# Fewer gather steps among the gate groups and eight modulation rows moved, in the second expert layer of a decoder trunk

## The chip, the cores and the metric

The kernel runs on one core of a Trainium2 chip. The metric is device time in microseconds, the median of several runs. The engines of the core are named as in the profile: PE is the matrix engine (PEld its weight load), DVE the vector engine, ACT the scalar engine, POOL the general-purpose engine, and SP issues transfers. Transfers are also issued from ACT and POOL; all run on the same 16 transfer engines.

## The reference

A small decoder trunk with 512 tokens of width 1024 and two layers. The first layer mixes tokens with a gated linear recurrence, the second with latent attention; each is followed by an expert layer ("peer"), which is what this case is about. Every sub-layer is normalised and modulated by shift, scale and gate vectors computed from a conditioning vector c.

```python
mod = (jax.nn.silu(c) @ ada_w[l] + ada_b[l])[:, None, :]
sh1, sc1, g1, sh2, sc2, g2 = jnp.split(mod, 6, axis=-1)
...
h = rmsnorm(x, norm_ffn_g[l]) * (1.0 + sc2) + sh2
x = x + g2 * peer(h, ...)

def peer(h, w_q, sub_keys, u_tab, v_tab):
    q = (h @ w_q).reshape(B, S, PEER_HEADS, 2, PEER_HALF)
    s = jnp.einsum('bshpd,hpnd->bshpn', q, sub_keys)
    v1, i1 = lax.top_k(s[..., 0, :], PEER_TOPK)
    v2, i2 = lax.top_k(s[..., 1, :], PEER_TOPK)
    ...
    idx = e1 * N_KEYS + e2
    g = jax.nn.softmax(cv, axis=-1)
    act = gelu(einsum('bcd,bchkd->bchk', hc, u_tab[ic]))
    out = einsum('bchk,bchkd->bcd', gc * act, v_tab[ic])
```

Each token picks 16 of 16384 experts in each of 8 heads, 128 experts in all. An expert is one row of u (a dot product with the token) and one row of v (added with the gated activation as its factor).

## The kernel before

Tokens are handled in four blocks of 128. For three of them (384 tokens) the expert layer is computed densely: the tables u and v are streamed in 128 tiles of 128 experts, PE multiplies every token with every expert, and a matrix of gates, zero where a token did not pick an expert, selects. The fourth block is computed by gathering: for each of its 128 picks a row of u and a row of v is fetched per token, and DVE does the arithmetic.

The function `peer(l)` runs for l = 0 and l = 1, in these stages:

- **Scoring.** Four rounds of query products (pq), key products (sc) and top-k searches on DVE. After each round some modulation rows are computed (`adas`, line 1181: six in the first layer, two in the second) and some u parts run on PE. In the last round the fourth block is decoded at once, so that gathering can begin.
- **u parts** (`u_part`). One streams a tile of u, splits it into a high part (whi, on ACT) and a low part (wlo, on DVE, line 165), runs 24 products of 384 columns on PE (lines 201 to 203) and keeps the activations (gact). They fill every stage until all 128 are done; 66 of them are parked in memory (gscr). Each of the 8 blocks of the width takes three products (high and low parts), for precision.
- **Gate groups** (`gate_group`, line 1009 on). 24 groups of 16 tokens. For each half group DVE builds two one-hot tiles (oo, line 1022) and their product with the gates (pr, line 1024); PE multiplies them (wps, 8 pairs per half group) into gate matrices; ACT evicts those and they are written to memory (wscr). u parts stand between the groups. Two more blocks are decoded on DVE during this stage.
- **Value tiles.** For each of 128 tiles t: the gates are read back (wt), the activations weighted (line 1239) and split (ah on ACT, al on DVE), the tile of v loaded and split (vh on ACT, vl on DVE), and 18 products of 512 columns accumulate on PE (acc). From tile 76 to tile 110 each tile also carries one u part.
- **Close.** The second layer's output is turned to token order, normalised and stored.

**Gather steps** (`gather_steps`, line 1441 on) are a generator of 256 steps for the fourth block. Each step fetches one row per token into a slot named grow (four slots) with an indirect transfer on POOL's queue (line 1451). The steps come in rounds of 32: sixteen with rows of u, each a dot product on DVE (line 1455), then sixteen with rows of v, each a scaled sum into gacc on DVE (line 1460, the very first one line 1458). `EARLY` of the 256 are taken among the gate groups: after group i the count is brought up to `EARLY * (i + 1) // 20`, so that it is complete after the twentieth of 24 groups. The rest is spread over the value tiles by weights (`plan`): in the second layer 0.2 for tiles 0 to 7, 0.6 for 8 to 75, 2.6 for 76 to 110, 1.0 for 111 to 125.

**Modulation rows** (`ada`, line 145 on). There are 112 rows of 128 outputs. For each one its weights are loaded (ada_raw, 512 KB) and DVE multiplies them with the conditioning vector and sums (ada_junk, line 153), into one column of mod. `self.todo` lists the rows that are left and `adas` takes the next ones. The last eight, 88 to 95, are the gate g2 of the second expert layer; their first reader is `token_major` at value tile 90. In the first layer the value tiles take a row at every third tile from 38 on, with its load on POOL's queue and into a grow slot.

What sets the order: each engine works through its own queue in order, and waits there on semaphores. The order in a queue is made when the program is built, by a scheduler that simulates a timeline and keeps to the data dependences and to the `issue_after` hints, which place an instruction behind a given one. So an edit at one place can shift the order of its neighbours.

Of the kernel before, what the change touches and what calls it, by code (L numbers as in the profile page):

```python
# [46 lines left out]
UDEC = 13  # L47
UEND = 7
QUIET = 4
EARLY = 74  # L50
HT = 8
RAWS = 4
GROWS = 4
# [30 lines left out]
class Trunk:  # L84
# [953 lines left out]
    def peer(self, l):  # L1038
        nc, io, tc = self.nc, self.io, self.tc
        nd = NB - 1  # L1040
        with ExitStack() as st:
# [67 lines left out]
            def u_part(after=None):  # L1109
                t = state["u"]  # L1110
                state["u"] = t + 1
                out = self.bank("u", True)
                hi, lo = self.wtile(io["uT"][l][t], KC, eng=nc.vector)
                with tc.issue_after(after) if after is not None else ExitStack():
                    for k, (bh, bl) in enumerate(h):
                        self.mm3(out[:, :ND], (hi[:, k, :], lo[:, k, :]), (bh[:, :ND], bl[:, :ND]), k == 0, k == KC - 1)
                if t < OWN:
                    gact[t] = self.x.rearrange("p k t -> p (k t)")[:, t * ND:t * ND + ND]
                elif LEAD - SPILL <= t < LEAD:
                    g = acts.tile([P, ND], F32, name="gsp", bufs=3)  # L1120
                    nc.scalar.activation(g, out[:, :ND], AF.Gelu)
                    nc.scalar.dma_start(self.gscr[l, t - (LEAD - SPILL)], g)
                    return
                else:
                    gact[t] = ring(t)
                nc.scalar.activation(gact[t], out[:, :ND], AF.Gelu)  # L1126

            gpool = st.enter_context(tc.tile_pool(name=f"gath{l}", bufs=1))
# [6 lines left out]
            done = 0  # L1135
# [4 lines left out]
            def decodes(bs):  # L1140
                for b in bs:
                    res = []
                    for _ in self.decode(dpool, cvs[b], cis[b], iu[b], res):
                        yield
                    if b == nd:
                        gsel.append(self.gather_index(gpool, l, *res))
                    else:
                        prep[b] = self.gate_prep(pool, *res)

            with tc.tile_pool(name=f"pq{l}", bufs=1) as pool:  # L1150
                for grp in range(4):
                    keys = pool.tile([P, 4, P], F32, name="keys", bufs=2)
                    nc.scalar.dma_start(keys, io["keysT"][l][:, 4 * grp:4 * grp + 4, :])
                    outs = []
                    wq = l * 16 + 4 * grp
                    if grp == 0:
                        outs = pq0
                    qs = []
                    for m in range(4):
                        if m >= len(outs):  # L1160
                            outs.append(self.bank("pq"))
                            self.lin(outs[m], self.wtile(io["w_pq"][wq + m], KC, eng=nc.vector), h)
                        q = pool.tile([P, T], F32, name="pq_s", bufs=5)
                        nc.scalar.activation(q, outs[m], AF.Copy)
                        qs.append(q)
                    for b in (nd, *range(nd)):
                        sc = self.bank("sc")
                        for m in range(4):
                            nc.tensor.matmul(sc[:, m * P:m * P + P], qs[m][:, b * P:b * P + P], keys[:, m, :],
                                             start=True, stop=True)  # L1170
                        for m in range(4):
                            last = self.topk_half(pool, sc[:, m * P:m * P + P], vs[b][:, 4 * grp + m, :],
                                                  iu[b][:, 4 * grp + m, :])
                        self.candidates(pool, vs[b], cvs[b], cis[b], 2 * grp, 2)
                        if grp == 3 and b == nd:
                            for _ in decodes((nd,)):
                                pass
                            gsteps = self.gather_steps(gpool, l, *gsel[0], hn)
                    self.hold = ()
                    with tc.issue_after(last):  # L1180
                        self.adas(6 if l == 0 else 2, pool)
                    for _ in range(UPQ[grp]):
                        u_part()
            with tc.tile_pool(name=f"gate{l}", bufs=1) as pool:
                nsg = P // TG
                steps = decodes(range(nd))
                for i in range(UDEC):
                    u_part()
                while 0 not in prep:
                    next(steps)  # L1190
                n0, nt = state["u"], nd * nsg
                ds = 0
                wlast, plast = [None, None], []
                for i in range(nt):
                    more = 1 if i >= nsg and i % nsg < nsg // 2 else 0
                    while state["u"] < n0 + (LEAD - UEND - n0) * (i + 1) // nt + more:
                        u_part(after=wlast[-2])
                    w, p = self.gate_group(pool, l, i // nsg, i % nsg, *prep[i // nsg])
                    wlast.append(w)
                    plast.append(p)  # L1200
                    while ds < 7 * (i + 2) // nsg:
                        next(steps, None)
                        ds += 1
                    with tc.issue_after(plast[max(0, i - 1)]):
                        while done < min(EARLY, EARLY * (i + 1) // (nt - QUIET)):
                            next(gsteps)
                            done += 1
                while state["u"] < LEAD:
                    u_part(after=wlast[-1])
# [71 lines left out]
            for t in range(P):  # L1281
                j = t + RING - 3
                if t >= OWN and j < P:
                    if j < LEAD:
                        gact[j] = ring(j)
                        nc.sync.dma_start(gact[j], self.gscr[l, j - (LEAD - SPILL)])
                    else:
                        u_part()
                if t == P - 2:
                    late = vp.tile([P, NSG, WG * TG], F32R, name="late", tag="wt").rearrange("p a b -> p (a b)")  # L1290
                pair = weigh(t), v_load(t)
                if acc is None:
                    acc = [[self.bank(f"acc{b}{f}") for f in range(2)] for b in range(nd)]
                if t < P - LAST:
                    for f in range(2):
                        grp["v"] = v_part(t, f, *pair)
                else:
                    held.append((t, pair))
                if l == 0 and t == 2:
                    self.positions(gpool)  # L1300
                if l == 0 and 36 <= t < 84 and t % 3 == 2:
                    with tc.issue_after(grp["i"].ins):
                        self.adas(1, gpool, 64, GROWS, nc.gpsimd, "grow")
                if t >= 20 and (t - 20) % 8 == 0 and (t - 20) // 8 < KC:
                    k = (t - 20) // 8
                    with tc.issue_after(vdma[t]):
                        nc.sync.dma_start(self.x[:, k, :], self.xscr[:, k, :])
                if l == DEPTH - 1 and t >= 26 and (t - 26) % 8 == 0 and (t - 26) // 8 <= KC:
                    with tc.issue_after(grp["v"]):
                        self.token_major((t - 26) // 8, g2)  # L1310
                if l == DEPTH - 1 and t == P - 12:
                    fg = hpool.tile([P, D], F32, name="fgrow", tag="h4")
                    with tc.issue_after(vdma[t]):
                        nc.sync.dma_start(fg, bass.AP(tensor=io["final_g"].tensor, offset=io["final_g"].offset,
                                                      ap=[[0, P], [1, D]]))
                with tc.issue_after(grp["i"].ins):
                    while done < min(total, int(goal[t] + 0.01)):
                        next(gsteps)
                        done += 1
# [26 lines left out]
            for t, pair in held:  # L1346
                last = v_part(t, 0, *pair)
            self.preload(AF.Sqrt, emit(0))
            rest, c = None, 0
            for q in range(2):  # L1350
                for i, (t, pair) in enumerate(held):
                    with tc.issue_after(last):
                        last = v_part(t, 1, *pair, 2 * q * P, 2 * P, rest)
# [3 lines left out]
                    for _ in range((0, 2, 1, 1, 1, 0)[LAST * q + i]):  # L1357
                        with tc.issue_after(last):
                            last = finish(c)
# [196 lines left out]
```

## Time and profile before

| | us |
|---|---|
| median of 3 runs | 2970.81 |
| the runs | 2964.76, 2970.81, 2972.43 |
| the profiled execution | 2963.21 |
| its span, first to last instruction | 2961.4 |

| stage of the second expert layer, in the profiled execution | us from the span's start |
|---|---|
| scoring | from about 1715 |
| first gather step's transfer | 1952 |
| gate groups | 1975 to 2247 |
| remaining u parts | to 2278 |
| value tiles, first to last product | 2278 to 2952 |

A profile is one execution. Its page gives the busy time of each engine and the chain of work that ended last. The table of windows gives busy time per stage. Views of groups, waits and the timeline show single instructions: their start, their duration, and what ended the idle time before them. Durations of instructions that follow each other overlap a little, so the distance between starts is the better measure of what an instruction costs its engine.

### The profile page before, as it was taken

The numbers are of one execution on the slowest core, as the hardware profiler recorded it, in microseconds if no ns is written. First come the engines' busy times: TensorE is split into PE (matmuls) and PEld (weight loads), VectorE is DVE, ScalarE is ACT, GpSimd is POOL, SyncE is SP. The second block draws the span as 40 slices with busy tenths as digits, with TensorE's granted clock in tenths as the row PEclk, the third lists the DMA queues.
The fourth block names the chain that finished last, engine by engine and source line by source line (L and its number), as shares of the span: only waits on it lengthen the run. The fifth ranks groups of instructions, "written<-read, shape, count | busy, mean of one in ns | idle before, by whom it ended". The sixth has DMA issues, their size and how long they took to land.

```text
span 2961.4 us, 43899 instructions
## 1 busy us (share of the span) xinstructions
PE 2874.9 (97%) x15680; PEld 2566.0 (87%) x15680; DVE 2559.4 (86%) x4887; ACT 1387.6 (47%) x2039; POOL 960.9 (32%) x718
## 2 busy tenths in 40 slices
PE   7999999989999999999999999999999999999998
PEld 5689898989888889998778799999989888899997
DVE  8989999999888878889878888999997777888888
ACT  4753245656343333333576742456655333333333
POOL 4000003645142234535434400015643111244542
PEclk9999999999999999999999999999999999999999
DMA  8544558999999999999323334369999999999996
GB/s 317 188 139 147 173 178 305 357 371 367 307 393 359 365 321 354 319 350 324 121 83 114 120 132 136 125 216 353 362 355 370 319 335 322 310 328 354 345 333 224
DMA packets 296219, 813.71 MB, mean 275 GB/s; under 512 B 33152, under 2 KB 130560, under 8 KB 289600
## 3 DMA queue, kind: packets, MB, share of 16 engines
q1 hardware_dynamic: 188928, 439.41, 43.4%
q0 software_dynamic: 78912, 287.34, 26.9%
q10 hardware_dynamic: 28160, 84.14, 7.3%
q8 instruction: 124, 2.03, 0.3%
q14 instruction: 95, 0.78, 0.1%
HBM read 727.44 MB, written 83.36 MB: 274 GB/s over the span
## 4 chain that ended last, share of the span: by engine, by line
PE 72%; DVE 15%; issue 5%; DMA 4%; POOL 2%; ACT 2%; ACTq 0%; DVEq 0%; SPq 0%; POOLq 0%
PE acc L202 11%; PE acc L203 11%; PE acc L201 11%; PE u L201 8%; PE u L202 8%; PE u L203 8%; DVE wlo L165 3%; POOL grow L1451 2%; DVE oo L1022 1%; DMA grow<-in_u_dram,idx 1%; DVE pr L1024 1%; PE pq L202 1%; PE pq L203 1%; DMA ada_raw<-in_adaw_dram 1%; PE pq L201 1%
## 5 line engine op out<-in xcount | busy, mean ns | idle before, releaser
L1451 POOL DMA_INDIRECT grow<-in_u_dram,idx x256 | 374.8, 1464 | 1099.2 <-DVE gdot L1455 404.4
L201 PE MATMUL u<-h,wlo 128*128 128x384 f32 x2048 | 692.8, 338 | 2.0 <-DVE wlo L165 1.0
L203 PE MATMUL u<-h,whi 128*128 128x384 f32 x2048 | 688.5, 336 | 0.0
L202 PE MATMUL u<-h,whi 128*128 128x384 f32 x2048 | 687.6, 336 | 0.0
L203 PE MATMUL acc<-vh,ah 128*128 128x512 f32 x1512 | 589.4, 390 | 0.0
L202 PE MATMUL acc<-vl,ah 128*128 128x512 f32 x1512 | 589.1, 390 | 0.0
L1451 POOL DMA_INDIRECT grow<-in_v_dram,idx x256 | 411.6, 1608 | 514.5 <-DVE gacc L1460 336.5
L201 PE MATMUL acc<-vh,al 128*128 128x512 f32 x1512 | 555.8, 389 | 0.0
L165 DVE TENSOR_TENSOR wlo<-raw,whi 128x1024 fp32r<-128x1024 f32 (+1 forms) x313 | 383.3, 1226 | 85.0 <-ACT whi L164 84.9
L165 DVE TENSOR_TENSOR vl<-vraw,vh 128x1024 fp32r<-128x1024 f32 x252 | 308.4, 1224 | 125.8 <-ACT vh L164 120.5
L164 ACT ACTIVATE whi<-raw 128x1024 fp32r<-128x1024 f32 (+2 forms) x362 | 352.4, 975 | 114.9 <-issue 33.2
L201 PEld LDWEIGHTS u<-h,wlo 128*128 128x128 f32 x2048 | 386.6, 189 | 6.1 <-ACT gact L1126 1.7
L202 PEld LDWEIGHTS u<-h,whi 128*128 128x128 f32 x2048 | 386.3, 189 | 2.7
L203 PEld LDWEIGHTS u<-h,whi 128*128 128x128 f32 x2048 | 385.8, 188 | 0.1
L203 PEld LDWEIGHTS acc<-vh,ah 128*128 128x128 f32 x1512 | 283.8, 188 | 59.2
L202 PEld LDWEIGHTS acc<-vl,ah 128*128 128x128 f32 x1512 | 283.8, 188 | 57.4
L201 PEld LDWEIGHTS acc<-vh,al 128*128 128x128 f32 x1512 | 283.8, 188 | 57.0
L1460 DVE SCALAR_TENSOR_TENSOR gacc<-grow,gdot,gacc 128x1024 f32<-128x1024 f32 x254 | 325.2, 1280 | 8.9 <-DMA grow<-in_v_dram,idx 7.8
L1455 DVE CUSTOM_DVE_ANT_0 grow<-grow,hn 128x1024 f32<-128x1024 f32 x256 | 309.7, 1220 | 20.9 <-DMA grow<-in_u_dram,idx 20.6
L164 ACT ACTIVATE vh<-vraw 128x1024 fp32r<-128x1024 f32 x252 | 264.6, 1050 | 97.0 <-issue 73.5
L164 ACT ACTIVATE ah<-gact 128x384 fp32r<-128x384 f32 x204 | 106.6, 523 | 390.0 <-PE acc L203 248.5
L1033 ACT ACTIVATE stg<-wps 128x512 f32<-128x512 f32 x192 | 185.0, 1120 | 40.4 <-PE wps L193 40.4
(417 smaller groups left out, 4342.9 us busy)
## 6 DMA issues: line engine op xcount, KB each, us to landing
raw<-in_uT_dram SPq DMA_DIRECT2D x256, 512.0 KB
vraw<-in_v_dram SPq DMA_DIRECT2D x256, 512.0 KB
wscr<-stg ACTq DMA_DIRECT2D x48, 1024.0 KB
wt<-wscr SPq DMA_DIRECT2D x42, 1024.0 KB
ada_raw<-in_adaw_dram SPq DMA_DIRECT2D x76, 512.0 KB
gscr<-gsp ACTq DMA_DIRECT2D x132, 192.0 KB
gact<-gscr SPq DMA_DIRECT2D x108, 192.0 KB
ada_raw<-in_adaw_dram POOLq DMA_DIRECT2D x36, 512.0 KB
```

What stands on the lines that cost most here:

```text
L164: last = nc.scalar.activation(hi, src, AF.Copy)
L165: lo = (eng or nc.vector).tensor_tensor(lo, src, hi.bitcast(F32), op=OP.subtract)
L201: nc.tensor.matmul(out, al, bh, start=first, stop=False, **kw)
L202: nc.tensor.matmul(out, ah, bl, start=False, stop=False, **kw)
L203: last = nc.tensor.matmul(out, ah, bh, start=False, stop=last, **kw)
L1022: nc.vector.tensor_tensor(oo.rearrange(by_pair, d=2), io, toks(et), op=OP.is_equal)
L1024: prod = nc.vector.tensor_tensor(pr.rearrange(by_pair, d=2), hot, toks(gp), op=OP.mult)
L1033: nc.scalar.activation(stg[:, :, c:c + 4].rearrange("p e t -> p t e"), wps.rearrange("p (t e) -> p t e", t=4), AF.Copy, scale=1.0 / GSCALE)
L1451: nc.gpsimd.indirect_dma_start(out=row, out_offset=None, in_=tabs[s], in_offset=bass.IndirectOffsetOnAxis(ap=idx[:, k:k + 1], axis=0))
L1455: nc.vector.tensor_tensor_reduce(row, row, hn, op0=OP.mult, op1=OP.add, scale=1.0, scalar=0.0, accum_out=col)
L1460: nc.vector.scalar_tensor_tensor(acc, row, col, acc, op0=OP.mult, op1=OP.add)
```

## The change

Three edits, all for the second layer (l = 1):

- `EARLY` becomes a pair: 74 for the first layer as before, 56 for the second. Eighteen gather steps are therefore taken in the value tiles instead of among the gate groups.
- The two modulation rows after each scoring round are dropped for l = 1.
- The value tiles of the second layer also take a modulation row at every third tile from 38 on, while there are any left (eight: tiles 38 to 59), with its load on POOL's queue and into a grow slot.

```diff
-EARLY = 74
+EARLY = (74, 56)
...
                     self.hold = ()
-                    with tc.issue_after(last):
-                        self.adas(6 if l == 0 else 2, pool)
+                    if l == 0:
+                        with tc.issue_after(last):
+                            self.adas(6, pool)
                     for _ in range(UPQ[grp]):
                         u_part()
...
                     with tc.issue_after(plast[max(0, i - 1)]):
-                        while done < min(EARLY, EARLY * (i + 1) // (nt - QUIET)):
+                        while done < min(EARLY[l], EARLY[l] * (i + 1) // (nt - QUIET)):
                             next(gsteps)
                             done += 1
...
                 if l == 0 and t == 2:
                     self.positions(gpool)
-                if l == 0 and 36 <= t < 84 and t % 3 == 2:
+                if 36 <= t < 84 and t % 3 == 2:
                     with tc.issue_after(grp["i"].ins):
-                        self.adas(1, gpool, 64, GROWS, nc.gpsimd, "grow")
+                        self.adas(1, gpool, (64, 112)[l], GROWS, nc.gpsimd, "grow")
```

## The prediction

> **What bounds the kernel now.** I read four views: the page for the whole, a table of windows cut at the stages of the second expert layer, the groups and waits of its gate stretch, and the timeline. The page first:
>
> ```profile
> PE 2874.9 (97%) x15680; PEld 2566.0 (87%) x15680; DVE 2559.4 (86%) x4887; ACT 1387.6 (47%) x2039; POOL 960.9 (32%) x718
> PE   7999999989999999999999999999999999999998
> GB/s 317 188 139 147 173 178 305 357 371 367 307 393 359 365 321 354 319 350 324 121 83 114 120 132 136 125 216 353 362 355 370 319 335 322 310 328 354 345 333 224
> PE 72%; DVE 15%; issue 5%; DMA 4%; POOL 2%; ACT 2%; ACTq 0%; DVEq 0%; SPq 0%; POOLq 0%
> ```
>
> PE carries the chain, with DVE close behind. But a share of the span does not say where an edit pays; the stages do. The table of windows of the second expert layer (columns: window, length, then busy time of each engine with its instructions in brackets, granted clock, share of the transfer engines, GB/s):
>
> ```profile
> core 0: us, PE busy (x) PEld busy (x) DVE busy (x) ACT busy (x) POOL busy (x), PEclk, DMA share, GB/s
> 1740.00:1890.00 150.00, 150.00 (x819) 138.56 (x818) 129.67 (x643) 46.12 (x62) 0.00 (x0) 1.00 0.41 130
> 1890.00:1920.00 30.00, 30.00 (x178) 30.00 (x177) 29.55 (x158) 14.81 (x19) 0.00 (x0) 1.00 0.33 106
> 1920.00:1950.00 30.00, 30.00 (x175) 30.00 (x174) 29.86 (x113) 15.66 (x21) 0.00 (x0) 1.00 0.46 144
> 1950.00:1975.00 25.00, 25.00 (x147) 24.93 (x146) 23.18 (x54) 14.67 (x21) 5.29 (x4) 1.00 0.80 270
> 1975.00:2247.00 272.00, 256.46 (x1932) 250.32 (x1930) 261.11 (x310) 169.53 (x211) 147.75 (x69) 0.97 0.95 348
> 2247.00:2278.00 31.00, 30.49 (x186) 30.45 (x187) 16.64 (x22) 13.78 (x20) 7.94 (x5) 1.00 1.05 365
> 2278.00:2574.00 296.00, 296.00 (x1319) 245.10 (x1318) 223.38 (x292) 109.73 (x153) 47.23 (x50) 1.00 0.94 326
> 2574.00:2887.00 313.00, 313.00 (x1579) 283.25 (x1578) 261.88 (x334) 115.49 (x157) 149.75 (x114) 1.00 0.94 337
> 2887.00:2961.00 74.00, 65.86 (x290) 53.94 (x288) 66.48 (x92) 28.99 (x51) 21.50 (x14) 0.96 0.61 226
> ```
>
> 1740 to 1890 is scoring: PE full, DVE with 20 us to spare. 1975 to 2247 holds the gate groups: the only long stage where PE is not full and DVE nearly is (261.1 of 272). From 2278 the value tiles run, cut here at tiles 72 and 112: PE full in both rows, DVE free for 73 and 51 us.
>
> How much does PE really lose in the gate stretch? A busy PE need not run at its pace, so I take the pace from starts. Timeline, one undisturbed piece, first and last of 32 gate products and of 45 u products:
>
> ```profile
> 2046.96 0.23 PE L1030 MATMUL wps<-pr,oo 128*128 128x128 f16 x1
> 2048.70 0.22 PE L193 MATMUL wps<-pr,oo 128*128 128x128 f16 x1
> 2049.41 0.33 PE L201 MATMUL u<-h,wlo 128*128 128x384 f32 x1
> 2057.04 0.34 PE L203 MATMUL u<-h,whi 128*128 128x384 f32 x1
> ```
>
> 31 steps in 1.74 us are 0.056 us each; 44 in 7.63 us are 0.1734. The tables of windows for tile u and for tile wps give the counts of the gate stretch:
>
> ```profile
> 1975.00:2247.00 272.00, 213.81 (x1174) 204.93 (x1172) 24.23 (x49) 0.97 0.95 348
> 1975.00:2247.00 272.00, 52.13 (x752) 88.68 (x93) 0.97 0.95 348
> ```
>
> 1174 x 0.1734 + 752 x 0.056 = 245.7 us. So PE loses 272 - 245.7 = **26.3 us**, 15.5 of it plainly idle, the rest below pace (the granted clock is 0.97 there). The stretch's waits of PE and of DVE name the cause:
>
> ```profile
> PE wps L1030 <- DVE pr L1024: 15.1, 7, 5.1
> DVE grow L1455 <- DMA grow<-in_u_dram,idx: 5.0, 3, 4.4
> DVE wlo L165 <- ACT whi L164: 3.8, 3, 2.7
> DVE oo L1022 <- PE wps L193: 2.1, 2, 1.2
> ```
>
> PE waits for pr, the gate product's operand that DVE makes; DVE itself waits 10.9 us in all. The stretch is bound by DVE.
>
> **The change part by part.** *Eighteen gather steps leave the gate groups.* The groups of grow in that stretch:
>
> ```profile
> L1455 DVE CUSTOM_DVE_ANT_0 grow<-grow,hn x37: 1212/1222/1227, 1982.4 to 2241.7; 128x1024 f32<-128x1024 f32 x37
> L1460 DVE SCALAR_TENSOR_TENSOR gacc<-grow,gdot,gacc x31: 1240/1281/1289, 2043.5 to 2222.3; 128x1024 f32<-128x1024 f32 x31
> ```
>
> Steps alternate 16 dots (L1455) and 16 sums (L1460). 74 steps end 10 dots into the third round, 56 end 8 sums into the second round: 8 sums and 10 dots leave. What a step holds DVE is its distance to the next start:
>
> ```profile
> 1983.58 1.22 DVE L1455 CUSTOM_DVE_ANT_0 grow<-grow,hn 128x1024 f32<-128x1024 f32 x1
> 1984.73 1.22 DVE L1455 CUSTOM_DVE_ANT_0 grow<-grow,hn 128x1024 f32<-128x1024 f32 x1
> 2910.54 1.28 DVE L1460 SCALAR_TENSOR_TENSOR gacc<-grow,gdot,gacc 128x1024 f32<-128x1024 f32 x1
> 2911.74 0.55 DVE L165 TENSOR_TENSOR al<-gact,ah 128x384 fp32r<-128x384 f32 x1
> ```
>
> 1.15 and 1.20 us, so 10 x 1.15 + 8 x 1.20 = 21.1 us, about one step per group, since the quota is spread over twenty groups. DVE's work falls to 261.1 - 21.1 = 240.0 us; with its 10.9 us of waits kept, 250.9. PE needs 245.7. The two bounds now lie 5 us apart, and work cut so finely does not interleave perfectly, so I take 254: **18 us gained**. The ends: 26.3 us (no PE loss left) and 6.4 (the loss falls only as the steps do, 26.3 x 18/74). The longest single wait should shrink too; DVE's timeline there:
>
> ```profile
> 1998.70 1.23 DVE L1455 CUSTOM_DVE_ANT_0 grow<-grow,hn 128x1024 f32<-128x1024 f32 x1 [4.43 <-DMA grow<-in_u_dram,idx]
> 2000.99 2.35 DVE L1024 TENSOR_TENSOR pr<-oo,gp 128x2048 f16<-128x2048 f16 x2
> ```
>
> A dot stood before pr and waited for a row, as the first two groups ask for seven rows of four slots. They will ask for five. What is late next is PE itself, or a remaining decode before pr.
>
> *Eight modulation rows leave scoring.* Each takes 1.28 us of DVE:
>
> ```profile
> L153 DVE CUSTOM_DVE_ANT_0 ada_junk<-ada_raw,csil,vecs x8: 1277/1280/1295, 1778.1 to 1938.3; 128x1024 bf16<-128x1024 f32 x8
> ```
>
> 10.2 us go from a stage where PE is full at 1.00 clock, so the cover is PE and I count nothing. The last two stand at 1935 and 1938, where DVE has no pause; decoding may end 2.5 us earlier. That can only shorten the first gate wait, within the 26.3. SP loses eight loads of 512 KB at a transfer share of 0.41: nothing.
>
> *Both arrive at the value tiles.* There 200 steps instead of 182 are spread by the weights, whose sum over the tiles is 148.4 (8 x 0.2 + 68 x 0.6 + 35 x 2.6 + 15 x 1.0): 0.81 a tile instead of 0.74 up to tile 75, 3.50 instead of 3.19 in tiles 76 to 110 (where u parts run too), 1.35 instead of 1.23 in 111 to 125. The rows take every third tile from 38 to 59. DVE gets 4.9 steps and eight rows by tile 72, 16 us into 73 free; 11.3 steps by tile 112, 13 us into 51 free, and is then busy 275 of 313, 88%. Each brings a transfer of 128 x 1024 x 4 bytes, 0.524 MB, on POOL's queue, busy 47 and 150 us of 296 and 313. A row's load takes a grow slot, so the next gather queues behind it on POOL, and vl and al behind it on DVE. Can PE keep its pace under that? The first layer already does this with 182 steps and 16 rows (here 200 and 8); its value tiles, up to tile 31, 71 and 111:
>
> ```profile
> 760.00:890.00 130.00, 130.00 (x575) 107.63 (x574) 113.45 (x164) 51.94 (x70) 44.44 (x30) 1.00 1.00 363
> 890.00:1054.00 164.00, 164.00 (x725) 135.84 (x724) 134.44 (x185) 59.42 (x82) 43.37 (x40) 1.00 1.00 364
> 1054.00:1365.00 311.00, 311.00 (x1561) 281.51 (x1560) 255.52 (x327) 112.39 (x154) 139.11 (x108) 1.00 0.93 332
> ```
>
> DVE at 87% in the first row, and PE full in all; its weights give up to 3.26 steps a tile, so 3.50 lies somewhat beyond. Second-layer traffic would be 326 + 12.9 x 0.524 MB / 296 us = 349 GB/s, then 337 + 11.3 x 0.524 / 313 us = 356. Only the 90 us of tiles 38 to 59 go higher: 9.6 transfers more, 326 + 56 = 382. The first layer's slice from 814 to 888 us moved 393 with PE at nine tenths or more. So I count **nothing**; the ends are nothing (PE is already full, no gain possible) and 41 us, the whole 26 transfers at 332 GB/s.
>
> *The end.* 1.8 more steps in tiles 111 to 125, 2.1 us of DVE, into a stretch where it works 66.5 of 74 us; the last sum must precede the last token block. I take 0.5 us, ends 0 and 2.1.
>
> Sum: -18 + 0 + 0 + 0.5 = -17.5 us. The profiled execution took 2963.2 us (span 2961.4), so 2945.7 on its scale; it lies 7.6 us under the median of three, 2970.8, the scale of the forecast: **2953.3 us**.
>
> **The rivals.**
>
> *Order, not load.* PE's waits come from single orders in DVE's queue (a dot whose row has not landed, a burst of decode) and survive. For it: the 4.43 us above. Against it: DVE waits 10.9 us in 272, while 21 us of work go. Gain 6.4 - 0.5: 2964.9 us.
>
> *Transfers bound the value tiles.* If they already run at what the queues deliver, each added transfer delays the value loads: 26 x 0.524 MB = 13.6 MB at 332 GB/s cost 41 us, against 18 gained: 2970.8 + 23 = 2993.8 us. It decides once the deliverable rate lies below 349 to 356; the gain is used up at about 344. For it: the share of 0.94. Against it: 363 and 364 in the first layer, and the value tiles' own waits of DVE on rows:
>
> ```profile
> DVE grow L1455 <- DMA grow<-in_u_dram,idx: 7.2, 8, 2.5
> ```
>
> *A cap in tiles 38 to 59 alone.* If nothing above the 364 GB/s of the first layer can be held for long, 382 is 18 too much for 90 us: 18 x 90 / 364 = 4.5 us, 2957.8 us. For it: both first-layer stages stop at the same figure. Against it: the slice of 393. The Trainium skill, "DMA: Bandwidth & Descriptors", section "Bandwidth", gives such a cap, a memory limit of about 358 GB/s for one core; by it the estimate is 24 x 90 / 358 = 6 us, 2959.3 us. The trace disagrees with that figure: two stages ran at 363 and 364 for 294 us with PE full.
>
> *The change does less than it says.* Were fewer than eight rows left, the value tiles would carry fewer; the eight L153 rows exclude it, and the first use of them is at tile 90, after 59.
>
> **How the numbers follow.** Forecast 0.60, the cap 0.06, order 0.20, transfers 0.10 (with half their price, no change, 0.04 more). The low end is the full 26.3 us below the lowest run shown, 2964.8: 2938.5. The high end takes in the order rival and a value stretch that gives some back: 2970. About 0.3%, 9 us, is what a measurement of this kernel can tell from no change. Faster 0.60 + 0.06 = 0.66, same 0.20 + 0.04 = 0.24, slower 0.10.
>
> **What would show it.** Right: the gate stretch near 254 us, its PE loss under 10 us, pr waits of PE near a third of 15.1; the value tiles from first to last product still 675 us with PE full; DVE near 88% in tiles 76 to 110. Wrong: pr waits that stay with DVE idle (order), or value tiles where PE waits for vl or al behind a grow or ada_junk that waits for DMA (transfers). A reordered DVE queue elsewhere in the layer would also break it.

## The result and the profile after

The changed kernel takes 2986.12 us (median of 5 runs, 2984.34 to 2993.76) against 2970.55 us before in the same comparison: a ratio of 1.0065, 95% interval 1.005 to 1.0081. It is slower. The forecast was 2953.3 us, the range 2938.5 to 2970, and 0.10 stood on slower.

The profiled execution of the changed kernel took 2993.76 us (span 2992.0), the slowest of its five. Of the 30.6 us between its span and that of before, 10.4 lie ahead of the second layer's first query product (1714.1 us before, 1724.5 after), where PE, DVE and POOL work in the same order in both traces: that is how executions differ, not the change. So I compare lengths of stages, cut at the first and last product of each kind:

| us | scoring (first pq to first wps) | gates and rest of u (to first acc) | value tiles (to last acc) | after the last product |
|---|---|---|---|---|
| before | 270.1 | 293.4 | 674.8 | 9.0 |
| after | 271.5 | 285.7 | 677.6 | 32.6 |
| difference | +1.4 | -7.7 | +2.8 | **+23.6** |

The gate stretch gained 7.7 us, the value tiles lost 2.8, and 23.6 appeared where nothing was before: behind the last product. The page of the changed kernel, engines and chain:

```profile
PE 2881.8 (96%) x15680; PEld 2571.9 (86%) x15680; DVE 2560.7 (86%) x4887; ACT 1389.3 (46%) x2041; POOL 949.8 (32%) x726
PE 73%; DVE 14%; issue 5%; DMA 4%; ACT 2%; POOL 2%; ACTq 0%; DVEq 0%; SPq 0%; POOLq 0%
```

On the page the two kernels cannot be told apart; the chain by engine moves by one per cent. The table of windows by stage can (columns as in the prediction):

```profile
1755.00:1900.00 145.00, 145.00 (x784) 133.68 (x783) 121.90 (x629) 43.00 (x58) 0.00 (x0) 1.00 0.34 110
1990.00:2252.00 262.00, 251.09 (x1926) 244.15 (x1925) 244.50 (x286) 166.36 (x207) 115.95 (x56) 0.99 0.93 340
2282.00:2578.00 296.00, 296.00 (x1318) 245.10 (x1317) 235.12 (x320) 109.18 (x151) 62.28 (x63) 1.00 0.96 343
2578.00:2891.00 313.00, 313.00 (x1578) 283.28 (x1577) 258.67 (x319) 114.72 (x158) 143.21 (x110) 1.00 0.93 331
2960.00:2992.00 32.00, 0.00 (x0) 0.00 (x0) 21.67 (x30) 7.25 (x21) 5.48 (x6) 0.57 0.52 185
```

The fourth row is the one to look at. Tiles 72 to 112 were to get 11.3 gather steps more; DVE does 319 instructions there against 334 before, and the transfers move 331 GB/s against 337. More was asked and **less** was done, with PE full all the time. The last row is where the missing steps are: 32 us without a product, DVE at work in 21.7 of them. DVE's timeline there, lines left out between:

```profile
2945.47 2.60 DVE L1461 SCALAR_TENSOR_TENSOR gacc<-grow,gdot,gacc 128x1024 f32<-128x1024 f32 x2
...
2964.11 3.98 DVE L1461 SCALAR_TENSOR_TENSOR gacc<-grow,gdot,gacc 128x1024 f32<-128x1024 f32 x3
2969.24 1.28 DVE L1461 SCALAR_TENSOR_TENSOR gacc<-grow,gdot,gacc 128x1024 f32<-128x1024 f32 x1 [1.16 <-DMA grow<-in_v_dram,idx]
2971.98 1.28 DVE L1461 SCALAR_TENSOR_TENSOR gacc<-grow,gdot,gacc 128x1024 f32<-128x1024 f32 x1 [1.45 <-DMA grow<-in_v_dram,idx]
2973.58 2.60 DVE L1461 SCALAR_TENSOR_TENSOR gacc<-grow,gdot,gacc 128x1024 f32<-128x1024 f32 x2 [0.32 <-DMA grow<-in_v_dram,idx]
2976.22 1.29 DVE L1392 TENSOR_TENSOR y<-gacc,csil 128x512 f32<-128x512 f32 x2
```

The last product starts at 2959.4; sums (L1461, L1460 before) run on to 2976.2, some of them waiting for their rows, and then the fourth block is still to be normalised and stored, 15.8 us with nothing beside it. Before the change the last sum started at 2934.2, so all of this lay beside PE. The chain of the last stretch agrees; it goes from a slot to a transfer to a slot (start, length, what):

```profile
2953.24 1.82 POOL grow L1452
...
2955.64 5.79 DMA grow<-in_v_dram,idx
...
2967.83 5.66 DMA grow<-in_v_dram,idx
...
2973.58 1.29 DVE gacc L1461
```

That the steps are late is not an accident of the last tiles. DVE works its queue in order, so counting the steps ahead of each tile's weighting (L1240) in the trace gives the order of that queue:

| steps ahead of the weighting of tile | 72 | 80 | 88 | 96 | 104 | 112 | 120 | 127 |
|---|---|---|---|---|---|---|---|---|
| before | 123 | 138 | 164 | 189 | 214 | 235 | 247 | 256 |
| after | 109 | 124 | 149 | 172 | 197 | 218 | 230 | 240 |

From tile 80 to 104 the weights ask for 24 x 3.5 = 84 steps; 73 stand there, fewer than the 76 of before. Sixteen are left behind the last weighting. That is the order as built, and the chip keeps up with it. In tiles 72 to 112 PE waits for nothing, and DVE waits for rows no longer than this (us in total, times, longest):

```profile
DVE grow L1456 <- DMA grow<-in_u_dram,idx: 2.3, 1, 2.3
DVE gacc L1461 <- DMA grow<-in_v_dram,idx: 2.2, 2, 1.5
```

The 2.8 us of the value tiles are the first of the late steps: PE stops twice after 2945, 2.4 us in all, for an `al` that stands behind sums in DVE's queue. Last, the waits of PE and DVE in the gate stretch:

```profile
DVE wlo L165 <- ACT whi L164: 10.9, 10, 3.1
PE wps L1030 <- DVE pr L1024: 8.0, 8, 3.9
DVE oo L1022 <- PE wps L193: 3.0, 2, 2.0
DVE grow L1456 <- DMA grow<-in_u_dram,idx: 1.7, 2, 1.0
```

PE's waits for pr fell from 15.1 to 8.0 us, but not to a third; DVE idles 17.5 of 262 us now.

### The profile page after: what moved, and what is told of

It is laid out like the page before. It is cut to its first block, busy times and chain, and to the rows that moved or that the text cites. A ratio compares the mean times of both kernels' runs of the same rounds, so it can differ in the third digit from the quotient of the medians.

```text
span 2992.0 us, 43923 instructions
## 1 busy us (share of the span) xinstructions
PE 2881.8 (96%) x15680; PEld 2571.9 (86%) x15680; DVE 2560.7 (86%) x4887; ACT 1389.3 (46%) x2041; POOL 949.8 (32%) x726
## 4 chain that ended last, share of the span: by engine, by line
PE 73%; DVE 14%; issue 5%; DMA 4%; ACT 2%; POOL 2%; ACTq 0%; DVEq 0%; SPq 0%; POOLq 0%
PE acc L203 11%; PE acc L202 11%; PE acc L201 11%; PE u L201 9%; PE u L203 9%; PE u L202 9%; DVE wlo L165 2%; POOL grow L1452 2%; DMA ada_raw<-in_adaw_dram 1%; PE pq L202 1%; PE pq L201 1%; PE pq L203 1%; PE wps L1030 1%; DVE ada_junk L153 1%; PE wps L193 1%
## 5 line engine op out<-in xcount | busy, mean ns | idle before, releaser
L1452 POOL DMA_INDIRECT grow<-in_u_dram,idx x256 | 357.0, 1394 | 1082.4 <-DVE gdot L1456 383.0
L1461 DVE SCALAR_TENSOR_TENSOR gacc<-grow,gdot,gacc 128x1024 f32<-128x1024 f32 x254 | 325.1, 1280 | 12.7 <-DMA grow<-in_v_dram,idx 11.6
```

What stands on the lines that cost most here:

```text
L1452: nc.gpsimd.indirect_dma_start(out=row, out_offset=None, in_=tabs[s], in_offset=bass.IndirectOffsetOnAxis(ap=idx[:, k:k + 1], axis=0))
L1461: nc.vector.scalar_tensor_tensor(acc, row, col, acc, op0=OP.mult, op1=OP.add)
```

## The experiments

All diffs are against the changed kernel; each ratio is to the kernel before, in the same comparison.

**The two halves apart.** `only_gather` moves the steps and leaves the rows in scoring; `only_rows` does the reverse.

```diff
 # only_gather
-                    if l == 0:
-                        with tc.issue_after(last):
-                            self.adas(6, pool)
+                    with tc.issue_after(last):
+                        self.adas(6 if l == 0 else 2, pool)
...
-                if 36 <= t < 84 and t % 3 == 2:
+                if l == 0 and 36 <= t < 84 and t % 3 == 2:
 # only_rows
-EARLY = (74, 56)
+EARLY = (74, 74)
```

> Theories for the 16 to 22 gather steps that the changed kernel still has to do when PE's last product ends. Order: DVE's queue was built with only about 3.1 steps a tile in tiles 76 to 110 although the quota is 3.5, so the steps stand behind the last tile's work before the chip starts. Ring: on the chip four slots with a round trip of 11.0 us allow only 0.36 steps per us. Transfers: the value tiles run at what the transfer engines deliver. Here the eight modulation rows are back in scoring and the 18 steps stay in the value tiles. Order: the queue as built has 11 steps behind the last weighting instead of 16, so about 5 x 1.5 us less at the end, 2978 us. Ring: the rows are far from the tiles that are short of slots, so nothing changes, 2986. Transfers: 8 of 26 transfers less, 13 us, 2973.

> The eight rows in the value tiles, but 74 steps among the gate groups as before. Order: one step behind the last weighting, so the end is as before, 2970 us within 5, if the rows cost nothing by themselves. Ring: the same. Transfers: 8 x 0.524 MB at 332 GB/s, 13 us, 2983.

`only_gather`: 2978.00 us, ratio 1.002 (1.0009 to 1.003); 11 steps behind the last weighting, 21.0 us after the last product. `only_rows`: **2962.72 us, ratio 0.9967 (0.9954 to 0.9979)**, 9.0 us after the last product, value tiles 674.8. So the moved steps make the tail; the rows alone make the kernel faster. What the halves gain in front, over scoring and gates together: 3.1 us the steps alone (563.5 to 560.4), 6.9 the rows alone (556.6), 6.3 both (557.2). Each value is from one execution, and kernels with the same queues differ by up to 3.6 us in this part (below), so whether the gains add cannot be told. The gate stretch of `only_rows`, then of `only_gather`, in the table of windows:

```profile
1986.00:2248.00 262.00, 251.00 (x1937) 244.20 (x1936) 257.93 (x303) 167.60 (x209) 154.29 (x67) 0.99 0.98 359
```

```profile
1988.00:2253.00 265.00, 251.22 (x1932) 244.84 (x1931) 245.32 (x288) 168.39 (x209) 125.42 (x56) 0.99 0.93 337
```

DVE is busy 257.9 of 262 us in the first and 245.3 of 265 in the second. With 12.6 us less of DVE's work the stretch is no shorter: DVE's load was not what bound it.

**Too few slots?** A step needs one of four grow slots. In the changed kernel's tiles 80 to 110 a slot's turn takes about 11 us (by the semaphores of the trace, on average 7.1 from the start of the issue to landing, 2.5 until DVE gets to it, 1.25 of work, 0.4 to the next issue): four slots make 0.36 steps per us, or 3.0 per tile of 8.36 us where 3.5 are asked. But 2.5 us of the turn are the row's wait for DVE, not DVE's for the row. `slots5` gives every fifth step a fifth slot.

```diff
+            if l == 1:
+                self.more = st.enter_context(tc.tile_pool(name="more", bufs=1))
...
-                    row = vp.tile([P, D], F32, name="grow", bufs=GROWS)
+                    self.turn += self.more is not None
+                    if self.turn % 5 == 1:
+                        row = self.more.tile([P, D], F32, name="growx")
+                    else:
+                        row = vp.tile([P, D], F32, name="grow", bufs=GROWS)
```

> The changed kernel with a fifth slot for the gather steps of the value tiles (it takes over the place of the first gate tile). Ring: 5 / 11.0 us = 0.45 steps per us, more than the 0.42 asked for, so the backlog goes and the time falls by some 22 us to 2964. Order: the queue as built still has 14 steps behind the last weighting (16 in the changed kernel), so 2983. Transfers: 2986.

2979.24 us, ratio 1.0031 (1.002 to 1.0043): 14 steps behind the last weighting instead of 16, 25.0 us after the last product instead of 32.6. From tile 80 to 104 stand 73 steps, as in the changed kernel, and a row now lies ready 5.1 us before DVE takes it. Most of the tail stays: slots were not what was short.

**Only the order of the queue?** `forced1` puts each tile's weighting behind the last step of the tile before, so the queue follows the weights; `forced5` adds the fifth slot.

```diff
-                with tc.issue_after(vls[t - 1]) if t >= 1 else ExitStack():
+                behind = marks.get(t - 1)
+                with tc.issue_after(vls[t - 1]) if t >= 1 else ExitStack(), tc.issue_after(behind) if behind is not None else ExitStack():
...
-                        next(gsteps)
+                        step = next(gsteps)
+                        if l == 1 and done < total:
+                            marks[t] = step
```

> The changed kernel with four slots, but the weighting of each tile stands behind the gather steps of the tile before in DVE's queue, so the queue follows the quota: 3.5 steps a tile in tiles 76 to 110 and one step behind the last weighting. Order: the chip keeps up, the value tiles last 677 us as before, the end after the last product falls from 32 to some 9 us, 2964. Ring: DVE has to wait for slots, 3.5 steps take 9.7 us instead of the tile's 8.3, 35 x 1.4 = 49 us more in the tiles and the end saved, about 3010. Transfers: 11 transfers at 332 GB/s are 18 us more in the tiles and the end saved, about 2982.

> The run before with DVE's queue held to the quota of 3.5 steps a tile lost 27 us in the value tiles. What holds the chip there: slots or transfers? Here the same queue order with a fifth slot. Ring: 5 slots over a round trip of some 10.5 us give 0.48 steps per us, above the 0.42 asked for, so the value tiles last 677 us again and the time is about 2965. Transfers: a slot more moves no byte faster, the tiles last 704 us as with four slots, about 2993.

`forced1`: 2993.42 us, ratio 1.0069 (1.005 to 1.0089). The order is as asked (155, 183, 211, 237 steps at tiles 88 to 112, one behind the last), the tail is gone (9.8 us) and the value tiles take 703.9 us instead. `forced5`: 2984.64 us, ratio 1.0051 (1.0035 to 1.0068), value tiles 698.0, 9.3 after them. The time only changed its place: in this order the tiles do not take 3.5 steps at PE's pace, with four slots or five. Neither kernel took the time that one of its theories gave. The 24 tiles 80 to 103 of four kernels, each in its own trace: before, after, `forced1`, `forced5`:

```profile
2629.00:2829.00 200.00, 200.00 (x1019) 182.16 (x1018) 169.20 (x207) 73.82 (x101) 96.88 (x75) 1.00 0.97 350
```

```profile
2633.00:2833.00 200.00, 200.00 (x1019) 182.11 (x1018) 164.72 (x209) 73.45 (x101) 93.21 (x72) 1.00 0.96 344
```

```profile
2628.00:2847.00 219.00, 210.20 (x1043) 190.19 (x1042) 177.16 (x229) 74.73 (x104) 112.01 (x83) 0.98 0.95 344
```

```profile
2628.00:2849.00 221.00, 211.32 (x1067) 191.43 (x1066) 179.73 (x227) 75.33 (x105) 109.52 (x82) 0.99 0.95 345
```

350, 344, 344, 345 GB/s at shares of 0.95 to 0.97: with 76, 73, 84 and 84 steps the transfers move about the same per us, and the forced kernels need some 20 us more. DVE and POOL have room (177 and 112 of 219 in `forced1`). Eight such tiles with 28 steps move 8 x (2 x 0.524 + 0.197) + 28 x 0.524 = 24.6 MB (u, v, gates, rows), in 8 x 8.36 us 368 GB/s; with the 25 of before 23.1 MB, 345. Where DVE stops in `forced1` (tiles 72 to 112, us in total, times, longest), and the one wait of ACT for a load of u:

```profile
DVE wlo L165 <- ACT whi L164: 21.2, 13, 5.4
DVE grow L1459 <- DMA grow<-in_u_dram,idx: 17.7, 13, 2.8
...
DVE gacc L1464 <- DMA grow<-in_v_dram,idx: 8.2, 8, 2.1
ACT whi L164 <- DMA raw<-in_uT_dram: 3.2, 1, 3.2
```

Rows hold DVE up for 25.9 us, and here the weighting, and with it PE, stands behind them; 24% of the chain of this stretch are transfers of rows. The loads of u and v are not late: by the semaphores they land about 8 us before ACT splits them, one load of u excepted. In `forced5`, with one row more under way, DVE waits 0.4 us for rows, u and v land some 9 us ahead, and no transfer stands in the chain of these tiles. Even so 23 us are lost. PE stops for DVE, DVE for ACT, ACT for PE:

```profile
PE acc L202 <- DVE al L166: 7.3, 4, 2.9
DVE vl L166 <- ACT vh L165: 27.6, 26, 3.3
DVE wlo L166 <- ACT whi L165: 24.9, 17, 4.4
DVE grow L1470 <- DMA grow<-in_u_dram,idx: 0.4, 1, 0.4
ACT whi L165 <- PE acc L204: 47.5, 15, 7.3
```

So the forced order costs time of its own, and these two kernels do not show that transfers limit the tiles.

**Transfers taken away.** `halfv` leaves out every second load of v and uses the tile before twice, so that the odd tiles are not computed with; the splits, products and steps all stay.

```diff
-                raw = self.wp.tile([P, D], F32, name="vraw", tag="raw", bufs=RAWS)
-                vdma.append(nc.sync.dma_start(raw, io["v"][l * P + t]).ins)
+                if l == 1 and t % 2:
+                    raw = grp["raw"]
+                    vdma.append(vdma[-1])
+                else:
+                    raw = grp["raw"] = self.wp.tile([P, D], F32, name="vraw", tag="raw", bufs=RAWS)
+                    vdma.append(nc.sync.dma_start(raw, io["v"][l * P + t]).ins)
```

> The changed kernel with four slots, but every second value tile of the second layer uses the v tile loaded for the one before, so 64 loads of 0.524 MB are left out (the v of odd tiles is not computed with). The work of PE, DVE and ACT is the same, and DVE's queue as built then follows the quota (255 of 256 steps before the last weighting, where the changed kernel has 240). Ring: four slots still cannot turn fast enough, the value tiles lengthen as in the forced run, to some 700 us, 2990. Transfers: with 0.26 MB less per tile the gathers land in time, the tiles last 675 us, the end after the last product is 9 us, 2963.

2966.10 us, ratio 0.9993 (0.9983 to 1.0002). Value tiles 675.1, after them 9.4, and the order follows the weights without being forced (154, 182, 210, 237; one step behind). Its tiles 80 to 103:

```profile
2631.00:2832.00 201.00, 201.00 (x1023) 182.86 (x1023) 177.98 (x227) 72.61 (x102) 119.74 (x84) 1.00 0.95 341
```

Four slots, all the steps that the weights ask for (83 from tile 80 to 104), PE full. Neither four slots nor DVE nor POOL keep these tiles from 3.5 steps at PE's pace. A slot's turn falls to 9.7 us because DVE takes a row 0.9 us after it has landed instead of 2.5; the landing itself still takes 7.0. DVE waits for rows more than in `forced1`, 30.9 us, and PE feels nothing of it:

```profile
DVE grow L1460 <- DMA grow<-in_u_dram,idx: 19.2, 17, 2.4
DVE gacc L1465 <- DMA grow<-in_v_dram,idx: 11.7, 18, 1.4
```

The loads, with the raw buffers that they fill, are the only edit, so it is because of them that the build holds the steps back; a run with more raw buffers, which would tell the two apart, was not made. Whether the chip could have run this order with all loads is not shown; no kernel here has that.

**Transfers added.** `late_rows` is `only_rows` with the eight rows in tiles 74 to 88 instead of 38 to 59.

```diff
-EARLY = (74, 56)
+EARLY = (74, 74)
...
-                if 36 <= t < 84 and t % 3 == 2:
+                if (36 <= t < 84 and t % 3 == 2) if l == 0 else (74 <= t < 90 and t % 2 == 0):
```

> As the run with the rows alone (2962.7 us), but the eight rows stand at tiles 74 to 88, where u parts run, instead of 38 to 59. If the price of a transfer depends on the tiles it falls into (some 346 GB/s are delivered in tiles 80 to 103 whatever is asked, and that is already asked there), eight transfers cost up to 8 x 0.524 MB / 346 GB/s = 12 us; the queue as built has 5 steps behind the last weighting, some 7 us of end: 2970 to 2975. If the value tiles had room anywhere, 2963 as before.

2970.10 us, ratio 1.0004 (0.9994 to 1.0013): 7.4 us above `only_rows`, five steps behind the last weighting, 13.6 us after the last product, 4.6 more than `only_rows`. The rest lies in the gate stretch, 288.3 us against 285.1, where the two kernels have the same queues. Eight rows that are free in tiles 38 to 59 cost about 0.6 us each in tiles 74 to 88. From tile 80 to 104 70 steps and five rows stand, as many together as `only_rows` has steps (75): a row displaces a step. A row takes a slot as well as a transfer; that it is not the slot, `slots5` (73) and `halfv` (83) say.

**The quota moved to where there is room.** Four kernels change the weights of the second layer (tiles 0 to 7, 8 to 35, 36 to 75, 76 to 110, 111 to 125; 0.2, 0.6, 0.6, 2.6, 1.0 in the change). `plan_g3` is `only_gather` with 0.6, 1.1, 1.1, 2.2, 0.7; `plan_d` the change with 1.2, 1.6, 1.0, 2.2, 0.8; `plan_r66` has `EARLY` 66 and 0.8, 1.2, 0.8, 2.2, 0.8; `plan_r74` has `EARLY` 74 and

```diff
-            plan = ((KC, 0.2), (36, (0.95, 0.6)[l]), (KC + SPILL + 2, 0.6), (tail, (2.8, 2.6)[l]), (P - 2, (0.4, 1.0)[l]), (P, 0.0))
+            plan = ((KC, (0.2, 0.6)[l]), (36, (0.95, 1.0)[l]), (KC + SPILL + 2, (0.6, 0.8)[l]), (tail, (2.8, 2.2)[l]), (P - 2, (0.4, 0.8)[l]), (P, 0.0))
```

> Rows in scoring, 56 steps among the gate groups, and the quota of the value tiles moved forward: weights 0.6, 1.1, 1.1, 2.2, 0.7, so 1.3 steps a tile up to tile 75 and 2.7 in tiles 76 to 110; the queue as built has every step before the last weighting. If the backlog at the end is the whole loss of moving the steps, the end falls from 21 to 9 us against the run with the steps alone (2978): 2966. If more transfers in tiles 8 to 75 slow PE there, the value tiles last longer than 677 us and the gain is less.

> The changed kernel (rows and 18 steps moved) with the quota moved forward: weights 1.2, 1.6, 1.0, 2.2, 0.8; the queue as built has 4 steps behind the last weighting instead of 16. If the backlog is the loss, the end falls from 32 to some 14 us, 2968. If the rows' and the steps' transfers together are too much for tiles 0 to 75, the value tiles last longer than 677 us.

> Rows moved as in the change, 66 steps among the gate groups, weights 0.8, 1.2, 0.8, 2.2, 0.8, so that no step is left behind the last weighting and tiles 76 to 110 get 2.65 steps, below what the transfers deliver. If moving steps out of the gate groups gains anything beyond what moving the rows gains, the time falls below the 2962.7 us of the rows alone, by up to 5 us. If the gate groups gain the same with 74 and 56 steps, as their 285.1 and 285.7 us say, 2962 to 2963.

> Rows moved, 74 steps among the gate groups, weights 0.6, 1.0, 0.8, 2.2, 0.8: only the place of the steps within the value tiles differs from the run with the rows alone. That run had no backlog, so nothing to gain: 2962.7 within 3 us. Slower if tiles 8 to 75 cannot take a third more gathers beside the rows.

| | us | ratio (95%) | value tiles | after |
|---|---|---|---|---|
| plan_g3 | 2964.19 | 0.9984 (0.9973 to 0.9995) | 674.8 | 9.0 |
| plan_d | 2972.16 | 1.0005 (0.9996 to 1.0015) | 681.0 | 11.7 |
| plan_r66 | 2970.34 | 1.0 (0.999 to 1.0009) | 681.0 | 9.0 |
| plan_r74 | 2964.69 | 0.9979 (0.9971 to 0.9988) | 674.9 | 9.0 |

`plan_g3` moves the same eighteen steps as the change and has no tail: it is where they go that costs, not that they go. From tile 80 to 104 the four kernels have 72 or 73 steps, though their weights ask for 58 to 63 there; no kernel with all loads and no forced order has more than 76. Tiles 8 to 71 of `plan_g3`:

```profile
2310.00:2570.00 260.00, 260.00 (x1160) 215.25 (x1159) 216.73 (x294) 96.61 (x134) 86.20 (x68) 1.00 0.98 360
```

`plan_r66` was forecast at 2962 to 2963 us and missed it. The 6 us that it and `plan_d` lose in the value tiles are another matter: three stops of PE (4.9 us together) where ACT's queue holds a copy of the layer's output ahead of the split of v that PE needs, an order of the build (the timeline of `plan_r66` shows it for one of the three); in `plan_g3` and `plan_r74` PE does not wait there at all. None of the four beats `only_rows`.

**Which rows help the gates?** `last_two` moves only the two rows of the last scoring round.

```diff
-EARLY = (74, 56)
+EARLY = (74, 74)
...
-                    if l == 0:
+                    if l == 0 or grp < 3:
                         with tc.issue_after(last):
-                            self.adas(6, pool)
+                            self.adas(6 if l == 0 else 2, pool)
```

> EARLY is 74 in both layers; only the two modulation rows of the last scoring round go to the value tiles (tiles 38 and 41), the six of the first three rounds stay in scoring as before the change. Moving all eight rows took 8.3 us from the gate stretch with the u parts behind it (293.4 to 285.1) and cost nothing elsewhere. Theory A (the last two rows stand on DVE among the decode of the fourth block; without them the decode and the first gather steps come 2.5 us earlier and the first gate wait, 5.3 us, goes): the whole gain, gates 285 to 286 us, ratio 0.996 to 0.998. Theory B (each row counts alike, through DVE's work or its 512 KB): a quarter of it, gates about 291 us, ratio 0.999 to 1.000. Theory C (only the order that the build happens to give): neither value, the single waits of PE elsewhere than in either kernel. Value tiles 675 us, last product to the end 9 us in all three.

2961.97 us, ratio 0.998 (0.9971 to 0.9989); gates 287.0 us, 6.4 less than before, where all eight rows gave 8.3. Theory A had 285 to 286, B 291. The queues of PE, DVE and ACT in this stretch are those of `only_rows`, and so are those of `late_rows` and `plan_r74` (but for one step at the end): with the same order the four stretches last 285.1 to 288.7 us. Within that spread two rows, 2.6 us of DVE, do what eight do. They stood on DVE in the middle of the fourth block's decode, whose indices start the first rows' transfers. DVE's first steps in `last_two`:

```profile
1987.27 2.35 DVE L1024 TENSOR_TENSOR pr<-oo,gp 128x2048 f16<-128x2048 f16 x2
1989.54 0.28 DVE L969 TENSOR_TENSOR g<-g,gsum 128x128 f32<-128x128 f32 x1
1989.74 1.22 DVE L1456 CUSTOM_DVE_ANT_0 grow<-grow,hn 128x1024 f32<-128x1024 f32 x1
1990.88 0.08 DVE L1456 DVE_READ_ACCUMULATOR2_ANT gdot<- 128x1 f32 x1
1990.88 1.22 DVE L1456 CUSTOM_DVE_ANT_0 grow<-grow,hn 128x1024 f32<-128x1024 f32 x1
```

The dots now run one behind the other without the wait of 4.43 us for a row, and stand behind pr. Counted from the first query product, the first row's transfer starts 0.9 us earlier than before the change (237.0 us instead of 237.9) and the first dot 2.1 us later (270.4 instead of 268.3). Whether the earlier rows or the changed order does it, these runs do not separate, since every edit also shifts the order. It is not the load: DVE is busy 257.8 of 264 us.

## Why the prediction was wrong

**The value tiles, counted at nothing: the step that failed.** The prediction let tiles 76 to 110 take 3.50 steps each at PE's pace, because PE, DVE and POOL have room for them. The room was there (`halfv`), but DVE's queue was not built that way: from tile 80 to 104 it has 73 steps where 84 were asked, 3.04 a tile, and the excess came as 2.8 us in the last tiles and 23.6 us behind the last product. The prediction's last line had named a reordered DVE queue as a danger, without a price. It also averaged the demand on the transfers over 313 us (337, then 356 GB/s) and set it against 363 and 364 of the first layer, rows from tiles without u parts. The third row quoted there, 332 with u parts, was the like for like, and it was passed over. In tiles 80 to 103 the kernel before already moved 350 GB/s, and no kernel of this study moved more than 352 there.

**The rival "transfers bound the value tiles", 0.10, came nearest**, in the direction and in naming the transfers, but it had the shape wrong, and its mechanism is shown in part alone. Its cost, 41 us as slower tiles, came as 2.8 us of tiles and 23.6 behind the last product. Its sign, PE waiting for vl or al behind a row that has not landed, is absent from tiles 72 to 112 of the changed kernel. What the runs show is that the build holds the steps back because of the loads or the buffers that these fill (`halfv`) and not for want of a slot (`slots5`); that its simulated timeline runs short of transfers is inferred from this. Whether the chip's transfers would have carried 3.5 steps a tile in a better order stays open: `forced1` waits for rows, `forced5` loses nearly as much without.

**The end, 0.5 us (0 to 2.1).** Its premise was named, that the last sum must precede the last token block, but it priced the instructions added and not their lateness. It measured 23.6.

**The gate stretch, 18 us.** It measured 7.7, or 6.3 with the 1.4 that scoring lost. Fewer steps alone gave 3.1, with 16 us less of DVE's work. "The stretch is bound by DVE" was the error: a busy share of 96% was read as a bound. `only_rows` has DVE at 98% and is 8.3 us shorter in this stretch (4.7 in the least of the kernels with the same queues). The rival "order, not load" forecast 6.4.

**Eight rows out of scoring, nothing.** At least half of the gain in front was there: by themselves the rows gave 6.9 us in `only_rows`, 3.3 in the least of the kernels with the same queues. The note that decoding may end earlier had the right place: `last_two` shows the worth of the last two rows, though the first row's transfer starts 0.9 us earlier and not 2.5. It should have been a term.

**A cap at 364 in tiles 38 to 59.** It fell. The same tiles after the change, 91 us:

```profile
2439.00:2530.00 91.00, 91.00 (x409) 75.36 (x408) 77.94 (x105) 33.71 (x48) 24.08 (x24) 1.00 1.02 376
```

376 GB/s with PE full. This step of the prediction was right: the rows cost nothing there.

## What to carry to other kernels

Before work is moved into a stretch, compare what its transfers would need with what they move *in that same mix*, not in a neighbouring stretch or as an average over several. Then count, in the queue of the engine that does the work, what stands ahead of each tile against what was asked: here PE stayed full and the stretch kept its length, and the excess showed only as work behind the last product. And a share near 100% of an engine is no bound until a run with less of its work is shorter by that work: here two early instructions on the way to the first rows were worth as much (`last_two`, 0.998) as eighteen steps (`plan_g3`, 0.9984).

## What the hardware showed unexpectedly

What the transfers moved with the engines they run on nearly always busy was not one number. Tiles 80 to 103, with three or four gathered rows and a u part each, moved 341 to 352 GB/s in every kernel of this study, at shares of 0.95 to 0.97 and whether PE was full or not. Tiles with about one gathered or loaded row and no u part moved 360 (`plan_g3`, 260 us, share 0.98) to 376 (after the change, 91 us, share 1.02), with PE full. That 352 is a limit of the first kind is not shown: where PE is full, the transfers move what the queues ask for. The Trainium skill, "DMA: Bandwidth & Descriptors", section "Bandwidth", gives about 358 GB/s as what one core gets when both cores that share the memory stream; this program runs on one core, and 360 to 376 lie above it. Whether the mix lowers the rate, by the gathers or by the loads beside them, was not tried.

A gathered row of 0.524 MB took 7.0 to 7.4 us from issue to landing in tiles 80 to 110 of all kernels looked at for it, with four slots or five and with half the loads of v gone, and 5.6 in the tail, where less is moved. Fewer loads did not make a row land sooner.
